# Layer 1's heads: eight state places, early rows, and gated rows and gates on other DMA queues

## The chip, the core and the metric

The kernel runs on one core of one Trainium2 chip. The metric is device time in microseconds, the median of several executions of the whole program. Five engines have a queue of instructions each, worked off in order: PE (TensorE), DVE (VectorE), ACT (ScalarE), POOL (GpSimd) and SP (SyncE, which in this kernel only issues DMAs). A DMA is issued by an instruction in one of the queues of SP, ACT or POOL.

## The reference

Two layers over 640 tokens: 512 of a new stream (the prompt) and 8 running streams of 16 (the sample). Layer 0 is stick-breaking attention, layer 1 gated linear attention (GLA) with four heads and, for each sample stream, a state that is read, used and written back. What matters here is layer 1:

```python
def gla_chunk(S, inp):
    q, k, v, g = inp
    b = jnp.cumsum(g, axis=1)
    b_last = b[:, -1]
    q_in = q * jnp.exp(b)
    a = jnp.einsum('bchd,bshd->bhcs', q_in, k * jnp.exp(-b))
    a = jnp.where(jnp.tril(jnp.ones((C, C), dtype=bool)), a, 0.0)
    o = jnp.einsum('bhcs,bshe->bche', a, v) + jnp.einsum('bchd,bhde->bche', q_in, S)
    S = jnp.exp(b_last)[..., None] * S + jnp.einsum('bshd,bshe->bhde', k * jnp.exp(b_last[:, None] - b), v)
    return S, o

def gla_mixer(h, w_in, w_a2, b_a, g_out, w_out, S0=None):
    q, k, v, r, a_lr = jnp.split(h @ w_in, [nk, 2 * nk, 2 * nk + nv, 2 * nk + 2 * nv], axis=-1)
    g = (jax.nn.log_sigmoid((a_lr @ w_a2 + b_a).astype(f32)) / GLA_TAU).reshape(B, T, GLA_HEADS, GLA_DK)
    S, o = lax.scan(gla_chunk, S0, ...)
    o = o * lax.rsqrt(jnp.mean(o * o, axis=-1, keepdims=True) + EPS) * g_out
    y = (o.reshape(B, T, nv) * jax.nn.silu(r.astype(f32))).astype(h.dtype) @ w_out
    return y, S.astype(h.dtype)
```

`w_out` is 2048 x 2048; a head gives 4 x 128 of its 2048 input rows.

## The kernel before, in words

Products are fp32 in three matmuls: both operands are split into a high and a low part (`halves`, L134 and L135: an ACT cast, then a DVE subtraction), and high x high, high x low and low x high are summed in PSUM. Only the stage of layer 1's heads changes, about 1964 to 2412 us of the span.

**What sets the order.** PE's order is written by the program as it is built: a modelled clock `pe["now"]` moves on with each matmul, and class `Side` weaves side lanes (Python generators) into a main stream. A lane yields `step(wait, tp, z, tiled)`: it goes on when the modelled clock has passed `wait` and the PSUM banks that it asks for are free; `side.after(wait, f)` calls `f` later by that clock; `until` advances the clock till a condition holds. So modelled microseconds decide where an instruction stands, and the chip decides how long it waits there. The other engines' queues follow the order of the calls, rearranged by a scheduler.

**Main stream of the stage.** `others` (L653) makes q and k of heads 1 to 3 in 12 pieces of 128 columns; ACT copies them out of PSUM (L1514, tile `pl`) and stores them (L1516). Then `share(g)` (L699) for g = 0 and 1 is the part of the output projection for head g: 4 column blocks x 5 token blocks, each with 4 rows `kt` and three matmuls a row, added up in tiles `y` (ACT copies at L707 for g = 0, DVE additions at L704 for g = 1). Behind the stage come the rest of the projection (L368) and L2004.

**The side lanes.** `decays` makes the decay factors of each head (L1638 on). `prompt_lane` runs 16 units (head, block of 128 tokens). `sample_lane` treats a head's eight states in four groups of four (dt, e): four products with the states (L1864, into `ps_z`), then for each state a product of keys and values (L1870) with which DVE updates the state (L1872); `leaves` stores the updated state (POOL), and 7 modelled us later `ask` loads the next wanted state into a free place (POOL, tile `s0`, printed `s`). There are `S0` = 7 places. A group's products are written 13 modelled us after the load of its last state was issued, or later.

**Gated rows.** At the end of a unit, and of a head's sample part, `leave` turns the normed result (four transposes, L1601), multiplies it with the gate r on DVE (L1602, in place in the gate's tile) and stores it to the DRAM tensor `og_d` (POOL, L78, printed `og<-gate`). Gates come from DRAM into the same tiles (POOL, `gate<-gr`), two places for the prompt, one for the sample. `fetches` reads the stored rows back, 128 x 640 for each `kt` (SP, tile `og_in`), and splits them into `ogh` and `ogl`; `share(g)` starts when the four rows of head g are split (`came["rows"]`). It asks for the first row once head 0 is through and the last q/k product has been copied out (`came["last"]`).

All POOL DMAs go through `move` (L78) and all SP DMAs through `load` (L71).

Of the kernel before, what the change touches and what calls it, by code (L numbers as in the profile page):

```python
# [8 lines left out]
F32 = mybir.dt.float32  # L9
F32R = mybir.dt.float32r  # L10
# [22 lines left out]
WR = 2  # L33
S0 = 7
GP = 2
# [6 lines left out]
def hybrid_step_kernel(ctx: ExitStack, tc: tile.TileContext, A: dict, O: list):  # L42
# [234 lines left out]
    class Side:  # L277
# [10 lines left out]
        def after(self, wait, what):  # L288

            self.due.append((pe["now"] + wait, what))  # L290
            self.due.sort(key=lambda x: x[0])

        def share(self, **bufs):
            self.free = {k: [0.0] * n for k, n in bufs.items()}
# [389 lines left out]

    def share(g, og, w, leave=None, at=None, first=None):

# [27 lines left out]

        w0, w1 = made(), made()
        for c in range(4):
# [786 lines left out]

    with tc.tile_pool(name="gl", bufs=1, reuse_waits="tile") as gl:
        came = {"plain": False, "last": False, "of": 0, "when": 0.0}

        def keep(dst, hh):
            t = []

            def leave(nt, pt):  # L1510
# [4 lines left out]
                if nt:  # L1515
                    nc.scalar.dma_start(out=dst[:, hh, :], in_=t[0])  # L1516
                    for h in range(1, GH):
                        if hh and dst is gk_d[h]:
# [5 lines left out]
                                 for n0, dst in ((256 * h, gq_d[h]), (NK + 256 * h, gk_d[h])) for hh in range(2)],  # L1524
                       lambda: came.update(plain=True))
        for _ in range(2):
# [28 lines left out]

        masked = [gl.tile([P, P], F32, name=f"aT{n}") for n in range(3)]
        for t in masked:
# [28 lines left out]
        def gate(h, t0, tag, bufs):  # L1586
            g = gl.tile([P, 4, P], F32, tag=tag, name="gate", bufs=bufs)
            move(g, gr_d[h][:, :, t0:t0 + P])
            return g
# [6 lines left out]

        def leave(h, t0, on, g):

            tp = bank("tp")
            for s in range(4):  # L1600
                turn_block(tp[:, P * s:P * s + P], block(on[:, P * s:P * s + P]), ident)  # L1601
            dve.tensor_tensor(g, tp.rearrange("p (s t) -> p s t", s=4), g, op=ALU.mult)  # L1602
            move(og_d[h][:, :, t0:t0 + P], g)

# [4 lines left out]
        def decays():  # L1609

            def weights(h):
                wa2 = gl.tile([96, 256], F32R, tag="wa2", name="wa2", bufs=2)
                load(wa2.bitcast(F32), wa2_d[:, 256 * h:256 * h + 256])
                yield step(4.0 if h else 8.0)
                return wa2
# [54 lines left out]
        def prompt_lane():  # L1670
# [25 lines left out]
            def leave_left():  # L1696
                nonlocal left
                u, on = left
                left = None
                h, c = units[u]  # L1700
                leave(h, P * c, on, gs.pop(u))
                side.after(5.0, lambda: fetch_gate(u + GP))
                if c == 3:
                    through["p"] = h + 1

# [93 lines left out]
        def sample_lane():  # L1799
# [12 lines left out]
            for h in range(GH):  # L1812
# [43 lines left out]
                for n in range(4):  # L1856
                    dt, e = n // 2, n % 2
                    group = [(h, e, dt, m) for m in range(4)]
                    while any(x not in states for x in group):
                        yield step(0.3)  # L1860
                    yield step(max(since, max(states[x][1] for x in group) + 13.0) - pe["now"], tiled=True)
                    for m in range(4):
# [17 lines left out]
                yield step(7.0, tp=1)  # L1880
                leave(h, NP, on, g)
                through["s"] = h + 1
                if h + 1 < GH:
                    yield step(4.0)
                    here = fetch(h + 1)

        def fetches():

            def free(kt):
                g, s = kt // 4, kt % 4  # L1890
                return came["plain"] and came["shares"] >= min(2, g if s > 1 else g - 1)

# [5 lines left out]

            for kt in range(10):
                while min(through.values()) <= kt // 4 or not came["last"]:  # L1900
                    yield step(0.5)
                if kt not in rows:
                    yield step(5.0)
                    ask_rows(kt)
                    if kt % 4 < 3 and kt < 9 and came["plain"]:
                        ask_rows(kt + 1)
                    yield step(4.0)
                while not free(kt):
                    yield step(0.3)
                n = 20 + 2 * kt % 12  # L1910
                og1[kt] = slot(n, name="ogh"), slot(n + 1, name="ogl")
                halves(*og1[kt], rows.pop(kt))
                if kt % 4 < 3 and kt < 9 and kt + 1 not in rows:
                    ask_rows(kt + 1)
                came["rows"], came["at"] = kt + 1, pe["now"]
                yield step(0.5)
# [4 lines left out]
        drive(others)  # L1921
        with tc.tile_pool(name="w4", bufs=1, reuse_waits="tile") as w4:
            ring3["pool"] = w4
            first = [wraw(w_of(0, 0, i), 2, 512) for i in range(2)]
            for g in range(2):
                side.until(lambda: came["rows"] >= 4 * g + 4 and pe["now"] > came["at"] + 2.0)
                drive(share(g, og1, w_out1, first=first))
                came["shares"] = g + 1
                first = [wraw(w_of(g + 1, 0, i), 2, 512) for i in range(2)]
            ring3["pool"] = None  # L1930
            parts = [split(r) for r in first]
            first = [wraw(w_of(3, 0, i), 2, 512) for i in range(2)]
            side.finish()

# [98 lines left out]
```

## Time and profile before

| | us |
|---|---|
| median of 3 runs | 2536.63 (2534.4 to 2538.53) |
| the profiled execution's own time | 2535.51 |
| its span | 2533.8 |
| the stage of layer 1's heads | 1964 to 2412 |
| PE matmuls L653, L699, L1864 (busy, in the stage) | 294.5, 191.8, 21.9 |
| DMA issues on POOL in the stage: s, s stored, gate, og | 64, 64, 20, 20 |

A row of waits reads "engine, what it was about to do, what ended the wait: us in total, times, longest". A row of the timeline reads "start, duration, engine, line, operation, out<-in, shapes, count", with the idle time ahead of it in brackets and what ended it. A row of a table by windows gives the window, its length, the busy time of PE, PE's weight loads, DVE, ACT and POOL with the number of instructions, then the granted TensorE clock (1.00 is full), the share of the 16 DMA engines that was busy, and GB/s.

### The profile page before, as it was taken

The numbers are of one execution on the slowest core, as the hardware profiler recorded it, in microseconds if no ns is written. First come the engines' busy times: TensorE is split into PE (matmuls) and PEld (weight loads), VectorE is DVE, ScalarE is ACT, GpSimd is POOL, SyncE is SP. The second block draws the span as 40 slices with busy tenths as digits, with TensorE's granted clock in tenths as the row PEclk, the third lists the DMA queues.
The fourth block names the chain that finished last, engine by engine and source line by source line (L and its number), as shares of the span: only waits on it lengthen the run. The fifth ranks groups of instructions, "written<-read, shape, count | busy, mean of one in ns | idle before, by whom it ended". The sixth has DMA issues, their size and how long they took to land. (4 is left out here: it accounts for less than half of the span.)

```text
span 2533.8 us, 43960 instructions
## 1 busy us (share of the span) xinstructions
PE 2429.8 (96%) x17561; PEld 2150.1 (85%) x17561; DVE 1581.8 (62%) x2565; ACT 995.2 (39%) x1730; POOL 163.6 (6%) x390
## 2 busy tenths in 40 slices
PE   7899999999999989999999989999999999979998
PEld 5589999999999989888887768999999988857776
DVE  5575555555656655766775678666676565555556
ACT  4342222222223334555442345333333554545223
POOL 0010000000000000000000000000000233342100
PEclk8899999999999999999999999999999999989999
DMA  9966666766654357777864655354434778785634
GB/s 346 327 209 212 223 214 198 241 218 205 219 186 123 113 187 233 260 246 243 267 209 124 214 172 169 96 148 123 125 105 119 212 238 255 217 278 184 228 111 147
DMA packets 469439, 503.13 MB, mean 199 GB/s; under 512 B 42730, under 2 KB 366450, under 8 KB 469106
## 3 DMA queue, kind: packets, MB, share of 16 engines
q1 hardware_dynamic: 446274, 436.60, 54.8%
q0 software_dynamic: 16048, 51.92, 6.1%
q10 hardware_dynamic: 6912, 11.80, 1.3%
q8 instruction: 138, 2.26, 0.4%
q14 instruction: 67, 0.55, 0.1%
HBM read 411.10 MB, written 89.13 MB: 197 GB/s over the span
## 5 line engine op out<-in xcount | busy, mean ns | idle before, releaser
L594 PE MATMUL ps_mm<-sums,wh 128*128 128x320 f32 x2752 | 613.7, 311 | 1.5 <-ACT wh L134 1.5
L594 PE MATMUL ps_mm<-h,wh 128*128 128x320 f32 x2064 | 461.8, 312 | 5.7 <-DVE u L600 4.6
L594 PEld LDWEIGHTS ps_mm<-sums,wh 128*128 128x128 f32 x2752 | 458.3, 188 | 10.4 <-issue 7.4
L594 PE MATMUL ps_mm<-sums,wl 128*128 128x320 f32 x1376 | 425.8, 309 | 0.7 <-DVE wl L135 0.7
L135 DVE TENSOR_TENSOR wl<-wr,wh 128x1024 fp32r<-128x1024 f32 x193 | 236.1, 1224 | 244.0 <-ACT wh L134 243.2
L594 PEld LDWEIGHTS ps_mm<-h,wh 128*128 128x128 f32 x2064 | 343.2, 188 | 21.8 <-issue 13.0
L134 ACT CAST wh<-wb 128x1024 fp32r<-128x1024 f32 x170 | 178.4, 1049 | 426.1 <-PE ps_mm L594 352.8
L134 ACT CAST wh<-wr 128x1024 fp32r<-128x1024 f32 x193 | 202.6, 1050 | 346.6 <-PE ps_mm L594 184.6
L594 PE MATMUL ps_mm<-h,wl 128*128 128x320 f32 x1032 | 319.2, 309 | 0.0
L653 PE MATMUL ps_mm<-h,wh 128*128 128x320 f32 x1152 | 265.2, 318 | 5.3 <-ACT pl L1514 3.1
L594 PEld LDWEIGHTS ps_mm<-sums,wl 128*128 128x128 f32 x1376 | 258.4, 188 | 1.0 <-DVE wl L135 1.0
L135 DVE TENSOR_TENSOR wl<-wb,wh 128x1024 fp32r<-128x1024 f32 x170 | 207.9, 1223 | 60.5 <-ACT wh L134 60.1
L653 PEld LDWEIGHTS ps_mm<-h,wh 128*128 128x128 f32 x1152 | 193.0, 189 | 21.7 <-issue 11.4
L699 PE MATMUL ps_mm<-wh,ogh 128*128 128x512 f32 x450 | 197.4, 439 | 4.2 <-DVE y L704 2.7
L594 PEld LDWEIGHTS ps_mm<-h,wl 128*128 128x128 f32 x1032 | 193.8, 188 | 0.0
L653 PE MATMUL ps_mm<-h,wl 128*128 128x320 f32 x576 | 178.5, 310 | 0.0
L699 PE MATMUL ps_mm<-wh,ogl 128*128 128x512 f32 x450 | 177.9, 395 | 0.3 <-DVE ogl L135 0.3
L699 PE MATMUL ps_mm<-wl,ogh 128*128 128x512 f32 x450 | 177.7, 395 | 0.0
L699 PEld LDWEIGHTS ps_mm<-wh,ogh 128*128 128x128 f32 x450 | 85.6, 190 | 29.6 <-issue 14.4
L653 PEld LDWEIGHTS ps_mm<-h,wl 128*128 128x128 f32 x576 | 108.8, 189 | 0.0
L699 PEld LDWEIGHTS ps_mm<-wh,ogl 128*128 128x128 f32 x450 | 85.0, 189 | 20.3 <-DVE ogl L135 0.7
L518 PE MATMUL ps_mm<-wh,h 128*128 128x512 f32 x252 | 93.4, 432 | 5.9 <-ACT h L134 2.8
(355 smaller groups left out, 3747.0 us busy)
## 6 DMA issues: line engine op xcount, KB each, us to landing
ar<-in_w_ada_dram SPq DMA_DIRECT2D x160, 512.0 KB
wb<-in_sb_w_in_dram SPq DMA_DIRECT2D x82, 512.0 KB
kc<-in_cache_sb_k_dram SPq DMA_DIRECT2D x64, 512.0 KB
vc<-in_cache_sb_v_dram SPq DMA_DIRECT2D x64, 512.0 KB
wr<-in_gla_w_in_dram SPq DMA_DIRECT2D x51, 512.0 KB
wb<-in_gla_w_in_dram SPq DMA_DIRECT2D x45, 512.0 KB
wr<-in_sb_w_in_dram SPq DMA_DIRECT2D x44, 512.0 KB
ar<-in_w_ada_dram SPq DMA_DIRECT2D x64, 256.0 KB
```

The costliest lines, as they stand in the source:

```text
L134: nc.scalar.copy(hi, x)
L135: (e or dve).tensor_tensor(lo, x, hi.bitcast(F32), op=ALU.subtract)
L518: mm(acc[a], l, by(l, r[:, e, :]), start=j == 0 and e == 0 and begun, stop=j == 7 and e == 1 and last)
L594: mm(acc, l[:, k, :], by(l[:, k, :], r), start=start and k == 0 and first, stop=k == 7 and last, skip_group_check=True)
L653: mm(acc[nt], l[:, k, :], by(l[:, k, :], r), start=k0 == 8 and k == 0 and first, stop=k0 == 0 and k == 7 and last)
L699: mm(acc, l, by(l, r[:, e, :]), start=i == 0 and e == 0 and first, stop=i == 1 and e == 1 and last)
```

## The change

1. `S0` is 8. The wait for a group is 9 modelled us after the load for 13, and its `tiled` step (which keeps a distance to other such steps) comes after the wait, in a step of its own.
2. `leave` stores the gated rows from ACT's queue, 2 modelled us after the multiply; what followed the store (the next gate, `through`) follows it still. Gates are loaded from SP's queue. POOL keeps the states, `vst` and `S`.
3. Rows 0 to 2 of head 0 are loaded 8 modelled us after head 0 is through, into the tiles of pool `w4` (row 2 in two parts), and split once all but the last piece of `others` is written. Row 3 and on are read as before, with slightly other waits.
4. `share(0)` is begun at that same point: its weights are loaded and the first half split there (`apart`), the second half when the share goes on.
5. To make room, two of the three tiles `aT` lie in buffers that have served, and `wa2` has one buffer for two.

```diff
@@ -31,7 +31,7 @@
 ZSCALE = 128 ** -0.5
 TOK = T // P
 WR = 2
-S0 = 7
+S0 = 8
 GP = 2
 NPAIR = HEADS // 2
 PLAIN = 2
@@ -682,7 +683,7 @@
 
     y_t = {}
 
-    def share(g, og, w, leave=None, at=None, first=None):
+    def share(g, og, w, leave=None, at=None, first=None, apart=False):
 
 
         src = w.rearrange("(kt p) n -> p kt n", p=P)
@@ -712,7 +713,10 @@
         def made():
             return [t.rearrange("p (a n) -> p a n", a=2) for t in split(raws.pop(0))]
 
-        w0, w1 = made(), made()
+        w0 = made()
+        if apart:
+            yield
+        w1 = made()
         for c in range(4):
             ws = [w0, w1]
             if c < 3:
@@ -1501,7 +1505,8 @@
         k0 = 4 * g + 2 * i
         return w_out1.rearrange("(kt p) n -> p kt n", p=P)[:, k0:k0 + 2, 512 * c:512 * c + 512]
 
-    with tc.tile_pool(name="gl", bufs=1, reuse_waits="tile") as gl:
+    with tc.tile_pool(name="gl", bufs=1, reuse_waits="tile") as gl, \
+            tc.tile_pool(name="w4", bufs=1, reuse_waits="tile") as w4:
         came = {"plain": False, "last": False, "of": 0, "when": 0.0}
 
@@ -1522,7 +1527,7 @@
 
         others = plain(h2, src, [(n0 + P * hh, keep(dst, hh)) for h in range(1, GH)
                                  for n0, dst in ((256 * h, gq_d[h]), (NK + 256 * h, gk_d[h])) for hh in range(2)],
-                       lambda: came.update(plain=True))
+                       lambda: upper())
@@ -1553,7 +1558,7 @@
             for n, (a, b) in enumerate(((0, 0), (0, 1), (1, 0))):
                 mm(out, l[a], by(l[a], r[b]), start=start and n == 0, stop=stop and n == 2, skip_group_check=True)
 
-        masked = [gl.tile([P, P], F32, name=f"aT{n}") for n in range(3)]
+        masked = [t[1].rearrange("p k r -> p (k r)")[:, :P] for t in (sh_t, sc_t)] + [gl.tile([P, P], F32, name="aT2")]
@@ -1585,7 +1590,7 @@
 
         def gate(h, t0, tag, bufs):
             g = gl.tile([P, 4, P], F32, tag=tag, name="gate", bufs=bufs)
-            move(g, gr_d[h][:, :, t0:t0 + P])
+            load(g, gr_d[h][:, :, t0:t0 + P])
             return g
 
         def values(h, a, tag, bufs):
@@ -1594,13 +1599,17 @@
                 load(v[e].bitcast(F32), gv_d[h][e][P * a:P * a + P, :])
             return v
 
-        def leave(h, t0, on, g):
+        def leave(h, t0, on, g, then):
 
             tp = bank("tp")
             for s in range(4):
                 turn_block(tp[:, P * s:P * s + P], block(on[:, P * s:P * s + P]), ident)
             dve.tensor_tensor(g, tp.rearrange("p (s t) -> p s t", s=4), g, op=ALU.mult)
-            move(og_d[h][:, :, t0:t0 + P], g)
+
+            def out():
+                nc.scalar.dma_start(out=og_d[h][:, :, t0:t0 + P], in_=g)
+                then()
+            side.after(2.0, out)
 
 
         ready, through = {}, {"p": 0, "s": 0}
@@ -1698,10 +1707,12 @@
                 u, on = left
                 left = None
                 h, c = units[u]
-                leave(h, P * c, on, gs.pop(u))
-                side.after(5.0, lambda: fetch_gate(u + GP))
-                if c == 3:
-                    through["p"] = h + 1
+
+                def then():
+                    side.after(7.0, lambda: fetch_gate(u + GP))
+                    if c == 3:
+                        through["p"] = h + 1
+                leave(h, P * c, on, gs.pop(u), then)
 
             def scores(u):
 
@@ -1858,7 +1869,8 @@
                     group = [(h, e, dt, m) for m in range(4)]
                     while any(x not in states for x in group):
                         yield step(0.3)
-                    yield step(max(since, max(states[x][1] for x in group) + 13.0) - pe["now"], tiled=True)
+                    yield step(max(since, max(states[x][1] for x in group) + 9.0) - pe["now"])
+                    yield step(0.0, tiled=True)
                     for m in range(4):
                         l = qz[e][:, dt, 32 * m:32 * m + 32]
                         mm(o[32 * m:32 * m + 32, :], l, by(l, states[group[m]][0]), start=False, stop=n == 3,
@@ -1878,17 +1890,46 @@
                 on = normed(o)
                 on = scaled_by(*on)
                 yield step(7.0, tp=1)
-                leave(h, NP, on, g)
-                through["s"] = h + 1
+                leave(h, NP, on, g, lambda: through.update(s=h + 1))
                 if h + 1 < GH:
-                    yield step(4.0)
+                    yield step(9.0)
                     here = fetch(h + 1)
+
+        begun = []
+
+        def upper():
+            came.update(plain=True)
+            begun.append(share(0, og1, w_out1, first=[wraw(w_of(0, 0, i), 2, 512) for i in range(2)], apart=True))
+            next(begun[0])
+
+        def row(kt):
+            n = 20 + 2 * kt % 12
+            og1[kt] = slot(n, name="ogh"), slot(n + 1, name="ogl")
+            return og1[kt]
 
         def fetches():
 
             def free(kt):
                 g, s = kt // 4, kt % 4
-                return came["plain"] and came["shares"] >= min(2, g if s > 1 else g - 1)
+                return came["shares"] >= min(2, g if s > 1 else g - 1)
+
+            while min(through.values()) < 1:
+                yield step(0.5)
+            yield step(8.0)
+            x = [w4.tile([P, 1024], F32, tag=t, name="og_in") for t in ("wh", "wl")]
+            for n in range(2):
+                load(x[n][:, :T], og_d[0][:, n, :])
+            load(x[0][:, T:], og_d[0][:, 2, :1024 - T])
+            load(x[1][:, T:2 * T - 384], og_d[0][:, 2, 1024 - T:])
+            while not came["plain"]:
+                yield step(0.3)
+            for kt in range(2):
+                halves(*row(kt), x[kt][:, :T])
+                yield step(0.8)
+            to = row(2)
+            halves(*[t[:, :1024 - T] for t in to], x[0][:, T:])
+            halves(*[t[:, 1024 - T:] for t in to], x[1][:, T:2 * T - 384])
+            came["rows"], came["at"] = 3, pe["now"]
 
             rows = {}
 
@@ -1896,20 +1937,19 @@
                 rows[kt] = gl.tile([P, T], F32, tag="pl", name="og_in", bufs=2)
                 load(rows[kt], og_d[kt // 4][:, kt % 4, :])
 
-            for kt in range(10):
+            for kt in range(3, 10):
                 while min(through.values()) <= kt // 4 or not came["last"]:
-                    yield step(0.5)
+                    yield step(0.3)
                 if kt not in rows:
-                    yield step(5.0)
+                    if kt > 3:
+                        yield step(5.0)
                     ask_rows(kt)
-                    if kt % 4 < 3 and kt < 9 and came["plain"]:
+                    if 3 < kt < 9 and kt % 4 < 3:
                         ask_rows(kt + 1)
                     yield step(4.0)
                 while not free(kt):
                     yield step(0.3)
-                n = 20 + 2 * kt % 12
-                og1[kt] = slot(n, name="ogh"), slot(n + 1, name="ogl")
-                halves(*og1[kt], rows.pop(kt))
+                halves(*row(kt), rows.pop(kt))
                 if kt % 4 < 3 and kt < 9 and kt + 1 not in rows:
                     ask_rows(kt + 1)
                 came["rows"], came["at"] = kt + 1, pe["now"]
@@ -1919,18 +1959,16 @@
         for x in (decays(), prompt_lane(), sample_lane(), fetches()):
             side.add(x)
         drive(others)
-        with tc.tile_pool(name="w4", bufs=1, reuse_waits="tile") as w4:
+        for g in range(2):
+            side.until(lambda: came["rows"] >= 4 * g + 4 and pe["now"] > came["at"] + 2.0)
             ring3["pool"] = w4
-            first = [wraw(w_of(0, 0, i), 2, 512) for i in range(2)]
-            for g in range(2):
-                side.until(lambda: came["rows"] >= 4 * g + 4 and pe["now"] > came["at"] + 2.0)
-                drive(share(g, og1, w_out1, first=first))
-                came["shares"] = g + 1
-                first = [wraw(w_of(g + 1, 0, i), 2, 512) for i in range(2)]
-            ring3["pool"] = None
-            parts = [split(r) for r in first]
-            first = [wraw(w_of(3, 0, i), 2, 512) for i in range(2)]
-            side.finish()
+            drive(share(g, og1, w_out1, first=first) if g else begun[0])
+            came["shares"] = g + 1
+            first = [wraw(w_of(g + 1, 0, i), 2, 512) for i in range(2)]
+        ring3["pool"] = None
+        parts = [split(r) for r in first]
+        first = [wraw(w_of(3, 0, i), 2, 512) for i in range(2)]
+        side.finish()
 
 
     share_banks(mm=8)
```

Left out: the one buffer of `wa2`, and a second sort in `Side.after` that changes nothing.

Three places where the order of the instructions moves. **PE, at the end of `others`** (`s_...` are states, `qz` queries, `vst` and `kst` values and keys of the sample, `on` a normed result, `wh`/`ogh` the high parts of weights and rows). Before:

```order
L653 MATMUL ps_mm<-h,wl 128x320
L1870 MATMUL ps_tp<-vst,kst_20578 128x512 x3
L1601 MATMUL ps_tp<-ident,on 128x128 x4
L1638 MATMUL ps_tp<-alr_in,wa_22802 128x320 x2
L1864 MATMUL ps_z<-s_23356,qz_20577 32x512
L1864 MATMUL ps_z<-s_23378,qz_20577 32x512
L1864 MATMUL ps_z<-s_23402,qz_20577 32x512
L1864 MATMUL ps_z<-s_23486,qz_20577 32x512
L1870 MATMUL ps_tp<-vst,kst_20579 128x512
L699 MATMUL ps_mm<-wh,ogh 128x512
L699 MATMUL ps_mm<-wl,ogh 128x512
```

With the change:

```order
L700 MATMUL ps_mm<-wh,ogh 128x512
L700 MATMUL ps_mm<-wl,ogh 128x512
L700 MATMUL ps_mm<-wh,ogl 128x512
L700 MATMUL ps_mm<-wh,ogh 128x512
L700 MATMUL ps_mm<-wl,ogh 128x512
L700 MATMUL ps_mm<-wh,ogl 128x512
L1876 MATMUL ps_z<-s_23266,qz_20579 32x512
L1876 MATMUL ps_z<-s_23329,qz_20579 32x512
L1876 MATMUL ps_z<-s_23347,qz_20579 32x512
L1876 MATMUL ps_z<-s_23370,qz_20579 32x512
L700 MATMUL ps_mm<-wh,ogh 128x512
L700 MATMUL ps_mm<-wl,ogh 128x512
```

Before, the group of states stood between the transposes of a prompt unit and the share's first products; now 15 share products stand ahead of it.

**POOL, around the states of head 2's last group** (`out_dram<-s` stores an updated state, `s_...<-in_state_gla_dram` loads one). Before:

```order
L78 DMA out_dram<-s_23227 128x512
L78 DMA gate<-gr_106 128x4x128
L78 DMA out_dram<-s_23339 128x512
L78 DMA og_93<-gate 512x1x128
L78 DMA s_23486<-in_state_gla_dram 128x512
L78 DMA s_23492<-in_state_gla_dram 128x512
```

With the change:

```order
L78 DMA out_dram<-s_22768 128x512
L78 DMA out_dram<-s_22783 128x512
L78 DMA s_23396<-in_state_gla_dram 128x512
L78 DMA out_dram<-s_22793 128x512
L78 DMA s_23411<-in_state_gla_dram 128x512
L78 DMA s_23440<-in_state_gla_dram 128x512
L234 TENSOR_TENSOR on_r<-on_ms,mhalf 128x1
```

The gates and the stores of gated rows are gone from between the states' stores and loads.

**ACT, at the last copies of q and k** (`pl<-ps_mm` is such a copy, `gk_102<-pl` its store). Before:

```order
L1514 COPY pl<-ps_mm 128x320
L1639 ACTIVATE b<-ps_tp,cols 128x320
L1516 DMA gk_102<-pl 128x640
L1639 ACTIVATE b<-ps_tp,cols 128x320
L1642 ACTIVATE b<-b 128x640
L134 CAST ogh<-og_in 128x640
```

With the change:

```order
L1519 COPY pl<-ps_mm 128x320
L1584 ACTIVATE on,oss<-ps_tp 128x512
L1857 CAST kst_20581<-ps_tp 48x512
L1521 DMA gk_102<-pl 128x640
L1766 ACTIVATE ps_tp<-ps_tp,ed 128x512
L1610 DMA og_93<-gate 512x1x128
L1588 ACTIVATE on<-ps_tp,on_r 128x512
L708 COPY y<-ps_mm 128x512
L134 CAST ogh<-og_in 128x640
L1648 ACTIVATE b<-ps_tp,cols 128x320
L1610 DMA og_93<-gate 512x1x128
```

Two stores of gated rows (L1610) now stand in this stretch, and copies of the share's first results (`y`, L708) stand ahead of and between the parts of the decays (`b`).

More of the change, by code (lines that the diff above doesn't have):

```diff
@@ L290, in after @@
             self.due.append((pe["now"] + wait, what))
+            self.due.sort(key=lambda x: x[0])
             self.due.sort(key=lambda x: x[0])
@@ L1611, in weights @@
             def weights(h):
-                wa2 = gl.tile([96, 256], F32R, tag="wa2", name="wa2", bufs=2)
+                wa2 = gl.tile([96, 256], F32R, tag="wa2", name="wa2")
                 load(wa2.bitcast(F32), wa2_d[:, 256 * h:256 * h + 256])
```

## The prediction

> **What bounds the kernel now.** I read the page first, then PE's waits in the changed stage, PE's timeline at the two long ones, the clock there, and last the queue that was late. The page:
>
> ```profile
> span 2533.8 us, 43960 instructions
> ...
> PE 2429.8 (96%) x17561; PEld 2150.1 (85%) x17561; DVE 1581.8 (62%) x2565; ACT 995.2 (39%) x1730; POOL 163.6 (6%) x390
> ```
>
> PE sets the time: 96% busy, 104 us idle. The change issues the same 15303 matmuls, so it can win idle time and time at a lowered clock, no more. What PE waited for from the heads of layer 1 to the end:
>
> ```profile
> PE ps_z L1864 <- DMA s<-in_state_gla_dram: 23.4, 3, 17.4
> PE ps_mm L653 <- ACT pl L1514: 3.1, 2, 1.6
> PE ps_tp L1566 <- DVE k L1664: 1.6, 1, 1.6
> PE ps_mm L368 <- DVE y L704: 1.5, 1, 1.5
> ```
>
> One wait stands out, that of the state products (L1864) for a sample state: 23.4 us in three pieces. The two that matter, in PE's timeline:
>
> ```profile
> 2170.20 1.92 PE L1864 MATMUL ps_z<-s,qz 128*32 128x512 f32 x2 [5.69 <-DMA s<-in_state_gla_dram]
> ...
> 2245.82 1.06 PE L1864 MATMUL ps_z<-s,qz 128*32 128x512 f32 x6
> 2264.32 1.92 PE L1864 MATMUL ps_z<-s,qz 128*32 128x512 f32 x2 [17.44 <-DMA s<-in_state_gla_dram]
> ```
>
> At 2245.82 three products of head 2's last group run and the fourth stands 17.44 us. Idle has a second price, the clock (column PEclk, ahead of the DMA share):
>
> ```profile
> 2168.00:2172.00 4.00, 1.80 (x2) 0.18 (x2) 0.82 (x1) 0.15 (x1) 1.07 (x2) 0.50 0.87 291
> 2172.00:2176.00 4.00, 4.00 (x19) 3.81 (x19) 1.64 (x5) 2.30 (x5) 1.03 (x2) 0.67 0.05 19
> 2248.00:2252.00 4.00, 0.00 (x0) 0.00 (x0) 2.92 (x5) 3.56 (x4) 1.48 (x3) 0.72 1.00 362
> ...
> 2264.00:2268.00 4.00, 3.68 (x6) 1.68 (x7) 0.81 (x2) 0.69 (x2) 0.75 (x1) 0.50 0.75 261
> 2268.00:2272.00 4.00, 4.00 (x14) 3.19 (x13) 2.34 (x4) 1.93 (x3) 2.12 (x4) 0.72 0.35 133
> ```
>
> Work done at a lowered clock costs its busy time times what is missing: 1.80 x 0.50 + 4 x 0.33 = 2.2 us behind the first wait, 3.68 x 0.50 + 4 x 0.28 = 3.0 behind the second. The waits and their shadows hold 23.4 + 5.2 = 28.6 us.
>
> Why the state was late stands in POOL's timeline:
>
> ```profile
> 2161.30 0.72 POOL L78 DMA_DIRECT2D og<-gate  x1 [6.08 <-DVE y L1640]
> ...
> 2251.60 0.76 POOL L78 DMA_DIRECT2D gate<-gr  x1 [1.57 <-issue]
> ...
> 2258.89 0.72 POOL L78 DMA_DIRECT2D og<-gate  x1 [5.99 <-DVE ogl L135]
> 2259.53 1.68 POOL L78 DMA_DIRECT2D s<-in_state_gla_dram  x3
> 2262.42 0.54 POOL L78 DMA_DIRECT2D s<-in_state_gla_dram  x1 [1.21 <-issue]
> ```
>
> The missing state is the first of the three loads at 2259.53. Ahead of it POOL held the store of gated rows 5.99 us; the earlier wait has the same picture (6.08). And it could not be asked sooner: with seven places and groups of four, a group's fourth state needs the place that the first state of the group before gives up.
>
> **The change, part by part.** Transfers of this stage (size, median us to landing):
>
> ```profile
> s<-in_state_gla_dram POOLq DMA_DIRECT2D x64, 256.0 KB, 4.8
> out_dram<-s POOLq DMA_DIRECT2D x64, 256.0 KB, 3.8
> ...
> gate<-gr POOLq DMA_DIRECT2D x20, 256.0 KB, 5.2
> og<-gate POOLq DMA_DIRECT2D x20, 256.0 KB, 3.8
> ```
>
> *Eight places.* The path from a freed place to its next state: update 0.75 (DVE, the row at 2267.00 below), issue 0.55 (POOL, 0.54 at 2262.42), store 3.8, issue 0.55, load 4.8: 10.4 us. With seven places, one of four states of a group has only the time from the previous group's updates to the next products, about 3.8 us on PE at head 2. With eight, a whole group is loaded while the other is used, and the distance is the time between groups. PE's new order puts 17 to 19 us of its own work (an estimate: its rows counted, at the durations of before) between the last update that frees a place of head 2's or 3's last group and that group's products: 7 to 9 us in hand. I take both big waits as gone, and what is left of the third kind (a few tenths to 5 us) as **1**, bounds 0 to 5. The shorter modelled wait (9 for 13) moves products forward and spends part of this margin; it is in that bound. What is late next is the work that stood behind the product:
>
> ```profile
> 2247.79 0.69 DVE L1602 TENSOR_TENSOR gate<-ps_tp,gate 128x512 f32<-128x512 f32 x1
> ...
> 2249.30 0.82 DVE L135 TENSOR_TENSOR ogl<-og_in,ogh 128x640 fp32r<-128x640 f32 x1
> ...
> 2261.14 0.83 DVE L135 TENSOR_TENSOR ogl<-og_in,ogh 128x640 fp32r<-128x640 f32 x1 [0.70 <-ACT ogh L134]
> ...
> 2267.00 0.75 DVE L1872 SCALAR_TENSOR_TENSOR s<-s,es,ps_tp 128x512 f32<-128x512 f32 x1 [4.83 <-PE ps_tp L1870]
> ```
>
> The fourth row of head 0, which the first out-projection products need, was split only at 2261.14 + 0.83 = 2261.97. Without the next part the big wait would shrink by 2264.32 - 2261.97 = 2.3 us and turn into a wait for rows.
>
> *Early rows and the early first weights.* The way of before's first row begins in SP's timeline:
>
> ```profile
> 2243.47 0.32 SPq L71 DMA_DIRECT2D og_in<-og  x1
> ```
>
> Three of the four rows are loaded and split before the last plain product; only row 3 comes on the old path. Between the last q/k product, which lets row 3 be asked, and its first use the new order has about 8.5 us of PE work (counted the same way), and the first row of before took from 2243.47 (issue) to 2249.30 + 0.82 = 2250.12 (split), 6.65 us: 1.9 us in hand.
>
> ```profile
> L135 DVE TENSOR_TENSOR wl<-wr,wh 128x1024 fp32r<-128x1024 f32 x193 | 236.1, 1224 | 244.0 <-ACT wh L134 243.2
> ...
> L134 ACT CAST wh<-wr 128x1024 fp32r<-128x1024 f32 x193 | 202.6, 1050 | 346.6 <-PE ps_mm L594 184.6
> ```
>
> The first weights' conversion lies under others, the second is made once the share resumes, for 1.05 on ACT and 1.22 on DVE; with the copies of y that ACT now makes beside the decays of head 3 I take **2** for the start of the share, bounds 0 (ACT and DVE are 39% and 62% busy) to 6.65 (row 3 late by its whole path).
>
> *Stores of gated rows on ACT, gates on SP.* POOL loses 20 + 20 issues of about 0.73 and 0.76, some 30 us, and what it stood before them:
>
> ```profile
> POOL gate L78 <- DMA og<-gate: 18.5, 6, 5.0
> ...
> POOL og L78 <- DVE gate L1602: 9.8, 7, 4.1
> POOL og L78 <- issue: 6.7, 4, 4.4
> POOL og L78 <- DVE y L1640: 6.1, 1, 6.1
> POOL og L78 <- DVE ogl L135: 6.0, 1, 6.0
> POOL og L78 <- DVE s L1872: 2.2, 1, 2.2
> ```
>
> 30.8 us before the stores and 18.5 before gates, 49.3 in all. Of the stores, ACT now issues each and stands until the multiply has ended. Queued behind it on ACT: copies of q and k and of y out of PSUM (PE needs the bank), conversions of weights, scales of states. The store is written 2.0 modelled us after the multiply, so that ACT mostly finds it done; at the big wait the multiply ended at 2247.79 + 0.69 = 2248.48, 10.4 us before POOL's store. I take **1** for ACT, bounds 0 (never in PE's way) to 30.8 (every hold passed on). For a gate SP stands until the old rows have landed; behind it are rows of v, weights and og rows, asked several us before use. I take **1**, bounds 0 to 18.5. No gain below nothing: PE waited for no gate and no og store elsewhere than counted.
>
> The Trainium skill ("Trainium Kernel Development and Optimization", section "Key Constraints") speaks against this part: DMAs of the SP, ACT and POOL queues run on the same 16 DMA engines, and issuing from several saves only the sequencer's issue time. The DMA share of 1.00 in the row at 2248 agrees that the engines were full there; by this rule the third part is worth its issues alone. Another page, "DMA: Bandwidth & Descriptors", section "SWDGE vs HWDGE vs iDMA", says that GpSimd's descriptor rings are SBUF state that VectorE can lock it out of; POOL's 5.99 us with the multiply long done would fit, and then the move frees POOL of more than its issues; no run here separates the two.
>
> *The tail.* Of the share's products 195 lie behind the last gated row, 213 before.
>
> ```profile
> 2397.42 13.23 PE ps_mm L699 x56
> ```
>
> At 13.23 / 56 = 0.236 us each that is 18 x 0.236 = 4.2 us less cover; PE starts the next section on weights and y, not on that row, with 1.5 us of waiting. I take 0, bounds 0 to 4.
>
> **Sum.** 28.6 - (1 + 2 + 1 + 1) = 23.6 us. Against the profiled run's 2535.5 (span 2533.8; the median is 1.1 higher): **2512**. About 0.2%, 5 us, is what a measurement here can tell from no change.
>
> **Rivals.**
>
> *A transfer limit.* At the big wait the engines were full (share 1.00), and the change takes no byte away; it starts 8 instead of 7 loads at once and adds early rows. If the transfers themselves are the limit there, the big wait stays in another form (a state, a row or weights that land late), and only the first wait goes, where the share was 0.87: 5.7 + 2.2 of clock = 7.9, so 2535.5 - 7.9 = **2528**. For it: the share. Against it: the missing state was asked late, not brought slowly (2259.53 to 2264.32 is 4.8, the median of all 64).
>
> *It does not do what it says.* The wait 13 to 9 moves the products forward by 4 modelled us, as much as a group's distance; if they then meet the same late loads, the eighth place is spent and the waits stay: 2535.5 - 0 = **2535**. Against it: PE's order shows the 17 to 19 us.
>
> *Slower.* The store on ACT is one instruction in a strict queue: it holds copies out of PSUM, and PE stands without a bank. The price is POOL's holds, handed to ACT and SP: 49.3 us. At full price 2535.5 - 28.6 + 49.3 = **2556**. It decides (slower than before by 0.2%) once more than 28.6 + 5 = 33.6 of the 49.3 reaches PE. For it: PE did wait for ACT's copies (L653, 3.1). Against it: most of POOL's holds stood for work that was late for POOL's place in the program only.
>
> **How the numbers follow.** Forecast 0.64, transfer limit 0.20, no effect 0.06, slower 0.10. The range: below, all four new costs at nothing, 2535.5 - 28.6 = 2506.9, and 2 for the runs' spread: 2505. Above, 2528 of the transfer limit and 2 for the runs' spread: 2530, which also holds the forecast with half of SP's bound or half of ACT's passed on (2512 + 9, 2512 + 15); beyond lie 0.16 of the other cases and a little of these two. Faster: 0.64 and 0.19 of the transfer limit, 0.83; same 0.07; slower 0.10.
>
> **What would show it.** Right: the row PE L1864 (now L1876) <- DMA s falls from 23.4 to under 5; no stretch near 2250 at clock 0.50; POOL's issue gaps of 6 us gone; 8 loads land before their group. Wrong: a new row PE <- ACT pl or y of more than 5 us (the slower rival), PE <- DVE ogl near the share's start (row 3 late), the state wait again with a landing above 10 us (the transfer limit), or the time at the median before.

## The result, and the profile after

The changed kernel takes **2514.0 us** (median of 4 runs, 2510.3 to 2514.8) against 2535.9 for the kernel before (median of 4): 0.9909 of it, 95% interval 0.9894 to 0.9924. That is 0.9% faster, 2 us beside the 2512 forecast and inside its range. The profiled execution took 2514.76.

The page of the changed kernel, span and busy time:

```profile
span 2513.0 us, 43986 instructions
...
PE 2427.7 (97%) x17561; PEld 2150.1 (86%) x17561; DVE 1580.6 (63%) x2566; ACT 994.1 (40%) x1731; POOL 135.2 (5%) x350
```

PE's waits from the heads of layer 1 to the end:

```profile
PE ps_mm L654 <- ACT pl L1519: 6.3, 1, 6.3
PE ps_mm L700 <- ACT y L708: 3.8, 2, 1.9
PE ps_mm L369 <- DVE y L705: 1.5, 1, 1.5
```

The row of the state products, 23.4 us before, is gone altogether. In PE's timeline, the group that had stood 17.44 us, and the stretches of the clock there:

```profile
2249.31 2.03 PE L1876 MATMUL ps_z<-s,qz 128*32 128x512 f32 x8
```

```profile
2248.00:2252.00 4.00, 4.00 (x18) 1.72 (x17) 2.53 (x4) 3.20 (x6) 1.09 (x2) 1.00 1.03 408
2252.00:2256.00 4.00, 4.00 (x20) 3.25 (x19) 3.10 (x8) 2.97 (x8) 1.08 (x2) 1.00 1.04 406
```

All eight products run in one go, PE is busy for the whole 4 us at full clock, and the 16 DMA engines are as full (1.03, 1.04) as when PE stood still.

To set the stage apart from the rest I take the time from its first q/k product that waited (1975.36 before, 1979.79 after) to the first product of L368/L369 (2413.01, 2392.24): **437.65 us before, 412.45 after**, 25.2 less. That the profiled executions differ by 20.75 comes of the part ahead of it, which the change does not touch: in the 14 profiled executions of this study that point lies anywhere from 1970.9 to 1979.8. In what follows this stage time stands beside the medians. PE in the stage, before and after:

```profile
1975.36:2413.01 437.65, 404.97 (x2292) 344.54 (x2293) 247.54 (x421) 213.82 (x390) 126.78 (x218) 0.97 0.73 230
1979.79:2392.24 412.45, 399.36 (x2292) 342.73 (x2293) 245.89 (x422) 212.34 (x391) 98.67 (x178) 0.99 0.76 244
```

For the same 2292 matmuls PE is idle 13.1 us where it was idle 32.7, 19.6 less, and busy 5.6 us less, at a mean clock of 0.99 for 0.97.

### The profile page after: what moved, and what is told of

Read it like the earlier page. It is cut to its first block, busy times and chain, and to the rows that moved or that the text cites. A ratio compares the mean times of both kernels' runs of the same rounds, so it can differ in the third digit from the quotient of the medians.

```text
span 2513.0 us, 43986 instructions
## 1 busy us (share of the span) xinstructions
PE 2427.7 (97%) x17561; PEld 2150.1 (86%) x17561; DVE 1580.6 (63%) x2566; ACT 994.1 (40%) x1731; POOL 135.2 (5%) x350
## 4 chain that ended last, share of the span: by engine, by line
PE 78%; DMA 6%; DVE 4%; ACT 3%; issue 1%; SPq 0%; POOL 0%; ACTq 0%; POOLq 0%; DVEq 0%
PE ps_mm L595 40%; PE ps_mm L700 9%; PE ps_mm L654 9%; PE ps_mm L369 3%; PE ps_tp L1086 2%; DMA gv<-kr 2%; PE ps_tp L1559 2%; PE ps_mm L519 1%; PE ps_tp L1046 1%; PE ps_tp L1138 1%; PE ps_z L1022 1%; PE ps_z L180 1%; PE ps_mm L2042 1%; PE ps_z L1100 1%; PE ps_z L222 1%
## 5 line engine op out<-in xcount | busy, mean ns | idle before, releaser
L595 PEld LDWEIGHTS ps_mm<-sums,wh 128*128 128x128 f32 x2752 | 457.9, 188 | 10.4 <-issue 7.4
```

The lines of the kernel that those rows point to most:

```text
L595: mm(acc, l[:, k, :], by(l[:, k, :], r), start=start and k == 0 and first, stop=k == 7 and last, skip_group_check=True)
```

## The experiments

All twelve in one table, with the two kernels. "Gates, og" is the queue of the gate loads and of the stores of gated rows; "wait" the modelled time from load to state products; "rows" whether rows 0 to 2 of head 0 are read early. Each ratio is to runs of the kernel before taken beside it, whose medians went from 2535.9 to 2539.2; so rows are better compared by their ratios than by their medians.

| kernel | places | gates, og | wait | rows | median us | ratio, 95% interval | stage us |
|---|---|---|---|---|---|---|---|
| before | 7 | POOL, POOL | 13 | late | 2535.9 | | 437.65 |
| changed | 8 | SP, ACT | 9 | early | 2514.0 | 0.9909 [0.9894, 0.9924] | 412.45 |
| e1 | **7** | SP, ACT | 9 | early | 2540.5 | 1.0000 [0.9991, 1.0009] | 440.27 |
| e2 | 8 | **POOL, POOL** | 9 | early | 2511.7 | 0.9893 [0.9876, 0.9909] | 414.46 |
| e3 | 8 | SP, ACT | 9 | **late** | 2525.1 | 0.9945 [0.9932, 0.9957] | 425.80 |
| e4 | 8 | POOL, POOL | 13 | late | 2543.4 | 1.0016 [1.0005, 1.0027] | 450.11 |
| e5 | 7 | SP, ACT | 13 | late | 2538.5 | 1.0001 [0.9991, 1.0012] | 441.80 |
| e6 | 8 | SP, ACT | 13 | late | 2539.9 | 1.0007 [0.9998, 1.0016] | 442.84 |
| e7 | 8 | POOL, POOL, later | 13 | late | 2534.6 | 0.9990 [0.9980, 0.9999] | 435.24 |
| e8 | 8 | **first 3 POOL, then SP**; ACT | 9 | early | **2505.3** | 0.9870 [0.9854, 0.9886] | 404.30 |
| e9 | 8 | POOL, ACT | 9 | early | 2515.1 | 0.9912 [0.9899, 0.9926] | 415.62 |
| e10 | e8 again | | | | 2505.2 (1 run) | | 408.52 |
| e11 | e8's | e8's | **13** | early | 2515.2 | 0.9916 [0.9900, 0.9932] | 417.34 |
| e12 | e8's | e8's, og 2 later | 9 | early | 2507.6 | 0.9888 [0.9873, 0.9903] | 413.20 |

My theory was the prediction's: the places end the state waits, the rows keep the hole from filling with the next wait, the queues matter little. Rivals: the queue move alone does it; the transfers are the limit.

**e1, seven places.**

```diff
-S0 = 8
+S0 = 7
```

> The changed kernel with seven state places for eight. If the eighth place is what took the state waits away (the forecast's reason), PE waits for DMA s at the state products again, 5 us or more in all, and the time rises from 2514 to 2519 or more. If the freed POOL queue alone did it (rival), the state waits stay under 1 us and the time within 3 us of 2514.

The whole gain is gone, more than expected, and not at the old place. PE's waits, and its timeline at the end of the stage:

```profile
PE ps_z L1876 <- DMA s<-in_state_gla_dram: 10.8, 4, 4.2
```

```profile
2382.75 1.06 PE L1876 MATMUL ps_z<-s,qz 128*32 128x512 f32 x6
2387.05 1.92 PE L1876 MATMUL ps_z<-s,qz 128*32 128x512 f32 x2 [3.24 <-DMA s<-in_state_gla_dram]
...
2408.53 1.91 PE L1876 MATMUL ps_z<-s,qz 128*32 128x512 f32 x2 [4.24 <-DMA s<-in_state_gla_dram]
...
2416.15 0.79 PE L369 MATMUL ps_mm<-wh,ogh 128*128 128x512 f32 x1 [0.78 <-DVE gate L1607]
```

The share's products are used up at 2382.75; the last three groups of states come behind them, each at the pace of its loads, for 33 us with hardly a product between. With seven places the chain of 64 states is the longest thing in the stage once the share starts sooner.

**e2, both transfers back in POOL's queue.**

```diff
-                nc.scalar.dma_start(out=og_d[h][:, :, t0:t0 + P], in_=g)
+                move(og_d[h][:, :, t0:t0 + P], g)
-            load(g, gr_d[h][:, :, t0:t0 + P])
+            move(g, gr_d[h][:, :, t0:t0 + P])
```

> The changed kernel with the stores of gated rows and the loads of gates back in POOL's queue. If eight places hide POOL's holds (7 to 9 us in hand against holds of up to 6), the state waits stay under 3 us, and the new wait for the copy of q (6.3 us at 2015, ACT's store behind an older DMA) goes with its 1.6 us of clock: 2508 to 2514. If POOL's holds were the cause of the late states whatever the places (rival), 10 us or more of state waits return: 2522 to 2535.

As expected under the theory: no state wait, 2511.7, not to be told from the changed kernel. The three longest rows of PE's waits:

```profile
PE ps_tp L1571 <- DVE k L1673: 4.2, 2, 3.8
PE ps_tp L1606 <- ACT on L1588: 3.1, 1, 3.1
PE ps_mm L654 <- ACT pl L1519: 2.8, 1, 2.8
```

The 6.3 for a copy of q is 2.8 again, and 7.3 us of waits for the heads' work have come in its place. So the queue move as made gains something and gives it back elsewhere; e8 and e9 take that apart.

**e3, late rows.** The early loads are taken out of `fetches` and its loop runs over all ten rows again:

```diff
-            for kt in range(3, 10):
+            for kt in range(10):
```

> The changed kernel with rows 0 to 2 of head 0 read on the old path, after the last plain product; the share is still begun early. If the rows are what stands next behind the states (forecast: split only 16 us after the last plain product), PE waits 10 to 17 us for ogl or the share's start and loses some 3 us to the clock: 2525 to 2534. If the rows were hidden anyway (rival), 2511 to 2517.

PE's waits:

```profile
PE ps_mm L700 <- ACT ogh L134: 15.0, 3, 10.4
```

The rows' own wait came, 15.0 us, and the stage is 13.4 us longer than the changed kernel's: the theory, not the rival.

**e4, the eighth place alone.** The kernel before, with

```diff
-S0 = 7
+S0 = 8
-                wa2 = gl.tile([96, 256], F32R, tag="wa2", name="wa2", bufs=2)
+                wa2 = gl.tile([96, 256], F32R, tag="wa2", name="wa2")
-        masked = [gl.tile([P, P], F32, name=f"aT{n}") for n in range(3)]
+        masked = [t[1].rearrange("p k r -> p (k r)")[:, :P] for t in (sh_t, sc_t)] + [gl.tile([P, P], F32, name="aT2")]
```

> The kernel before with the eighth place alone (and the buffers that make room for it); POOL's queue, rows and waits as before. Forecast's reason: the 5.7 us wait and its 2.2 of clock go, the 17.4 shrinks by 2.3 and becomes a wait for rows: 2535.5 - 10 = about 2525. If the places alone do nothing because POOL's holds set when a state lands (rival): 2533 to 2538, with 15 us or more of waits for DMA s.

Neither: the state waits fell to 0.7 us, and the time did not fall. PE's waits, and POOL's timeline at the longest:

```profile
PE ps_tp L1601 <- ACT on L1583: 26.9, 4, 13.8
```

```profile
2257.64 0.72 POOL L78 DMA_DIRECT2D og<-gate  x1 [2.45 <-issue]
...
2265.36 0.56 POOL L78 DMA_DIRECT2D s<-in_state_gla_dram  x1 [2.17 <-DMA og<-gate]
2265.91 0.56 POOL L78 DMA_DIRECT2D out_dram<-s  x1
2266.49 0.57 POOL L234 TENSOR_TENSOR on_r<-on_ms,mhalf 128x1 f32<-128x1 f32 x1
```

PE now waits for a normed result, whose factor `on_r` POOL makes 0.57 us long behind a line of DMAs that each stood; ACT came to the result at 2268.32, 1.3 us after `on_r` was done. That looked like POOL's queue being the next bound; e6 and e7 were to test it.

**e5, the queue move alone, and e6, eight places and the queue move.** The kernel before with `leave` and `gate` as changed (e5), and with e4's edit as well (e6).

> The kernel before with the queue move alone (gated rows stored from ACT, 2 later, gates loaded from SP; seven places, rows as before). If POOL's hold of 6 us ahead of the late state was its cause (as the prediction read POOL's timeline), the 17.4 shrinks by some 6 us and the 5.7 goes: 2522 to 2530. If the seventh place is the bound (e1 lost the whole gain with the queues moved), the state waits stay above 15 us in all or return elsewhere: 2531 to 2545.

> The kernel before with the eighth place and the queue move, without early rows, early weights and the shorter wait. e4 stood 26.9 us for the normed result, whose factor on_r is made on POOL behind held DMAs. If POOL's queue is the cause, that wait falls under 5 us and what stays is the wait for rows: 2522 to 2532. If eight places cost PE something else (rival), 2538 or more.

Nothing gained in either. PE's waits, of e5:

```profile
PE ps_mm L699 <- ACT ogh L134: 11.0, 2, 7.3
PE ps_mm L653 <- ACT pl L1514: 6.5, 1, 6.5
PE ps_z L1870 <- DMA s<-in_state_gla_dram: 5.0, 4, 2.3
```

and of e6:

```profile
PE ps_tp L1601 <- ACT on L1583: 20.1, 3, 12.8
PE ps_mm L653 <- ACT pl L1514: 4.3, 1, 4.3
```

In e5 the state waits did fall, from 23.4 to 5.0, with seven places. That fits POOL's holds as a cause of the late state, but does not show it alone: the order moved too, and head 2's last group now stands at 2268.36, behind the share's first products. Rows (11.0) and the copy of q took the place of the state waits. In e6 the wait for the normed result stayed with POOL's queue relieved, so **my reading of e4 fell**, as far as POOL was to be the only cause: in e6 `on_r` ended at 2261.3 and ACT came to the result only at 2264.92, behind a row's cast and the decays of head 3.

**e7, as e6 with both transfers in POOL's queue, written later.**

> As e6, but the stores of gated rows and the loads of gates stay in POOL's queue, only written later (2, 7 and 9 modelled us). If the place in POOL's order was what held on_r in e4, this is within 4 us of e6 and the wait for the normed result is under 8 us. If the queue itself is what matters (its gaps put to issue, 100 us in e4 and 5.8 with the change), it is like e4: 2538 to 2546, with 15 us or more of that wait.

Not as either had it: 19.6 us of that wait, as in e6, at 2534.6. Against e4 (26.9, 1.0016) writing the transfers later in the same queue is worth some 7 us by the ratios. In this hole ACT does stand 2.31 us for `on_r`, which ended at 2261.6: here POOL's queue is the last of the chains, in e6 ACT's, and the waits are of one size (12.7 and 12.8).

What e4 to e7 have in common is the place. The long wait behind the last plain product ends at 2264.3 before (a state), 2269.1 in e4 (normed result), 2262.5 in e5 (rows), 2265.7 in e6 and 2262.4 in e7 (normed result); counted from the start of the stage that is 289, 293, 291, 291 and 285 us. It is one hole in PE's program: when q and k are done, PE has no product left that does not hang on head 0's rows, on head 3's decays or on the last unit's result, and whichever of these chains or the state is taken away, the next one ends within some 4 us of it. One thing the four traces share: in the hole ACT stands at the cast of a row of head 0 until the row has landed, 4.11 us in e4 (to 2261.38), 4.73 in e5 (to 2256.36), 2.82 in e6 (to 2261.93) and 3.65 in e7 (to 2250.13), and the decays or the normed result come behind that cast in its queue. So a part of what PE's waits call the normed result is the wait for rows under another name.

The first wait of the kernel before (5.69 at 2170) is gone in e4, e6 and e7 too, but in its place PE stands 6.39, 4.98 and 6.39 us near 2091 for another normed result. Its `on_r` was done 3 to 4 us before ACT came to it, behind the decays of the next head.

**e8, the first three gates from POOL; e10, the same again** (its label names another edit, the kernel is e8's).

```diff
-            load(g, gr_d[h][:, :, t0:t0 + P])
+            (move if h == 0 and t0 in (0, P, NP) else load)(g, gr_d[h][:, :, t0:t0 + P])
```

> The changed kernel with the first three gates of head 0 loaded from POOL as before; all later gates from SP. The changed kernel stood 6.3 us at 2015 for a copy of q: ACT was held 6.7 us at its store of q until an earlier DMA of SP's had landed, behind three more DMAs of SP's. If those three gates are the cause, that wait is about 3 us as before the change, its 1.6 us of clock go, and the time is 2507 to 2512. If it only comes of where the eight state loads fall (rival), the wait stays at 5 to 7 us and the time at 2514.

> A second look at e8, for the trace alone: if its gain over the changed kernel is the start of the stage, the wait for a copy of q near 2007 is 1 to 3 us again and the stage from its first q/k product to the rest of the projection takes 402 to 407 us, where the changed kernel took 412.

The start of the stage in ACT's timeline, first the changed kernel, then e8:

```profile
1995.10 0.42 ACT L1519 COPY pl<-ps_mm 128x320 f32<-128x320 f32 x1
...
2002.59 0.33 ACTq L1521 DMA_DIRECT2D gq<-pl  x1
2002.95 1.28 ACT L1651 ACT_TABLE_LOAD   x1 [7.00 <-DMA v<-gv]
```

```profile
1988.14 0.42 ACT L1519 COPY pl<-ps_mm 128x320 f32<-128x320 f32 x1
...
1988.59 0.33 ACTq L1521 DMA_DIRECT2D gq<-pl  x1
1989.01 1.28 ACT L1651 ACT_TABLE_LOAD   x1
```

ACT's store of q stood until 2002.59 for an older load of v from SP's queue; in e8 it goes at once. The wait for a copy of q is 1.5 us in e8 and 3.8 in e10 (2.3 and 1.5), without a lowered clock behind it. Both came out a little beside what was expected: e8 is under its 2507 to 2512, and e10's stage, 408.52, is over its 402 to 407. The median is 2505.3, and the intervals of e8 and the changed kernel do not meet: **the best version of the study**, 1.3% under the kernel before. Its stage is 4 to 8 us shorter than the changed kernel's (408.52, 404.30 against 412.45), of which the start accounts for 4 to 6.

**e9, all gates from POOL, gated rows still from ACT.**

> The changed kernel with all loads of gates in POOL's queue, the stores of gated rows still on ACT. e2 (both in POOL's queue) gave 2512, e8 (only the first three gates there) 2505. If the gates are what makes POOL's gaps (20 loads in rows of 512 bytes that wait for older DMAs), it stands near e2: 2509 to 2514, with 20 us or more of POOL's idle put to issue. If the stores are, near e8: 2503 to 2508.

POOL's waits, of its loads of gates:

```profile
POOL gate L78 <- DMA og<-gate: 26.3, 6, 6.9
POOL gate L78 <- issue: 22.6, 7, 4.9
```

2515, 1 us above the range for gates as the cause of the gaps, and far from the other: POOL stands 40.4 us "for issue" in all its rows (22.6 of it before gates), against 13 in e8, and the stage is 7 to 11 us longer than e8's. Not all of it is POOL's: the waits for a copy of q are 4.5 us there.

**e11, e8 with the wait of 13 again; e12, e8 with the stores 2 later and the next gate 2 sooner after them.**

```diff
-                    yield step(max(since, max(states[x][1] for x in group) + 9.0) - pe["now"])
+                    yield step(max(since, max(states[x][1] for x in group) + 13.0) - pe["now"])
```

```diff
-            side.after(2.0, out)
+            side.after(4.0, out)
-                    side.after(7.0, lambda: fetch_gate(u + GP))
+                    side.after(5.0, lambda: fetch_gate(u + GP))
```

> e8 with a group's products written 13 modelled us after its last load again, for 9. If the shorter wait brings what the places allow (groups follow each other sooner, so that the last ones end under the share's cover), the last groups of states meet PE without cover and it loses 3 to 15 us: 2508 to 2520. If the wait is only margin (rival), 2503 to 2508.

> e8 with the stores of gated rows written on ACT 4 modelled us after the multiply, for 2, and the next gate 5 after that, for 7. If ACT's hold at the store (2.1 us before a copy of y, PE 1.9 behind it) is what is left of the queue move's price, the waits for y fall from 3.0 to under 1.5 and the time is 2502 to 2505. If it only moves the hold, 2504 to 2508.

e11 lost 10 us, a size that was expected, but not in the way that was expected: no row of PE's waits names a state. The longest is

```profile
PE ps_tp L1854 <- DVE kc L1849: 5.2, 3, 4.2
```

and 4.2 of it stand at 2238.47, in the hole again. ACT's timeline there shows why `kc` is late:

```profile
2236.63 0.72 ACT L134 CAST ogh<-og_in 128x640 fp32r<-128x640 f32 x1 [3.94 <-DMA og_in<-og]
2237.26 0.29 ACT L1848 CAST kc<-kd 128x128 fp32r<-128x128 f32 x1
```

ACT stands 3.94 us for the load of head 1's first row, and `kc` is cast behind it. Why the longer wait moves the order so that this shows was not looked into. All of PE's waits from 1964 on add up to 16.1 us in e11, 7.8 in e8 and 10.5 in e10. e12 gained nothing; its waits for `y` are 3.9 us, and a new one came:

```profile
PE ps_mm L700 <- ACT y L708: 3.9, 3, 1.9
PE ps_tp L1882 <- DVE s L1884: 2.4, 1, 2.4
```

So moving the store does not shorten those waits; what sets them stays open.

## Why the prediction was right, point by point

**The gain of 28.6 us** (waits 23.4, clock 5.2) was right: the row is gone and the clock in that stretch is 1.00. As to its cause, more than one thing would have ended the state waits: the places alone (e4, 0.7 us left) and the queue move alone, with the order that comes with it (e5, 5.0 left), nearly do. Neither shortened the program.

**What is late next** was the step that decided, and it held. Rows split at 2261.97 were to leave 2.3 of the 17.44 us; e4 to e7 end the same hole at 2262 to 2269 and stand between 0.9990 and 1.0016 of the kernel before. Early rows are worth 13.4 us of the stage (e3) with everything else in place. What the step did not see is that the normed result of the last prompt unit and head 3's decays hang in the same place and end as late as the rows. The margin of 1.9 us for row 3 rests on a misread row: the load at 2243.47 is that of head 0's second row; the first was asked at 2233.18 and split at 2243.44, 10.3 us and not 6.65. In the changed kernel row 3 took 8.9 us (asked 2229.26, split 2238.18), and its first product stands at 2240.15, so it was in time by 2.0.

**Eight places: residual 1** (bounds 0 to 5), measured 0. That they were necessary e1 shows, but by another way than the 10.4 us against 3.8: the written order puts the late groups behind the share, and the price is 27.8 us of the stage, not a remainder of the old wait.

**The shorter wait** I treated as a cost inside that bound. It is a gain: e11 puts it at 9 to 13 us of the stage (417.34 against 408.52 and 404.30). The sum takes for granted that nothing new comes late in the hole, and e11 shows that this holds with the wait of 9 and not with 13. By e11 the changed kernel with 13 would stand near 2524, an estimate; neither that kernel, nor early rows, the shorter wait or the early start of the share alone in the kernel before, was tried. That the time came out 2 us from the forecast is in this part luck.

**Start of the share: 2.** PE waits 3.8 for `y` and 0.3 for `wl`, where before it waited 0.9: 3.2.

**ACT 1 and SP 1** were mis-sized, and at a place not thought of. POOL's holds of 49.3 did go to SP:

```profile
SPq L71 <- DMA og<-gate: 99.2, 17, 13.5
```

99.2 us, where POOL stood 18.5 before gates, yet no row of PE's waits names a gate or a gated row. The cost was at the start of the stage, where three gates in SP's queue put ACT's store of q behind a load of v: 6.3 of wait instead of 3.1, and work at a lowered clock behind it:

```profile
2015.10:2019.00 3.90, 3.90 (x17) 3.90 (x18) 2.51 (x5) 3.87 (x5) 0.00 (x0) 0.59 0.44 122
```

3.90 x 0.41 = 1.6, together 4.8 where 2 stood. The sum of the stage by these terms is 28.6 - 3.2 - 4.8 = 20.6, and 25.2 were measured. Of the 4.6 between, 2.0 are the waits for `k` (1.6) and `on` (0.4) of the kernel before, which the new order has lost. Another 2.0 lie in PE's busy time, 5.6 us less where the clock terms give 5.2 - 1.6 = 3.6, and 0.6 in gaps that no row of waits names. The new costs were set too low (8.0 for 5), and what was not counted made up for it: that is luck too.

**The rivals.** *A transfer limit*: refuted by the two windows of the changed kernel above, where the DMA engines are full and PE is busy all the time. *It does not do what it says*: wrong, the longest state wait is gone. *Slower*: the sign set for it, a row PE <- ACT `pl` of more than 5 us, did come (6.3). Its whole price, 4.8, is far under the 33.6 at which that rival decides, and the other handed-over holds stayed off PE's path. The profile counts 17561 matmuls before and after; the prediction's 15303 stands in no view.

By the Trainium skill's rule ("Trainium Kernel Development and Optimization", section "Key Constraints") that issuing from several queues saves only the issue time, the queue move would be worth nothing to PE here. e2 against the changed kernel agrees (2511.7 and 2514.0). With the start mended, e8 is 6 us under e2, where the intervals overlap, and 10 under e9, where they do not; POOL's idle put to issue falls from 53.5 (e2) and 40.4 (e9) to 13. So against e9 moving the gates is worth something to PE; that it is this idle time is not shown, for e5 and e6 have as little of it and gain nothing.

## What to carry to other kernels

Where PE stands with nothing else to do, look for all the chains that end in that hole before valuing the one that the trace names: here the eighth place alone, the queue move alone and the two together gave nothing, and with early rows, the early start of the share and the shorter wait 0.9%. Give the engine work for the hole (early rows), and a longer ring where the ring sets the pace of what comes after. When DMAs move to another queue, look at whose counters they take: a store on ACT stood behind a load that SP had issued.

## What the runs showed of the hardware that was not expected

An ACT store issued in 0.33 us stood 6.7 us (1995.94 to 2002.59) until a load from SP's queue had landed, although it reads nothing of it. The trace keeps the number of the counter (semaphore) at which each DMA reports its landing: in this program those of SP and ACT take 100 to 105, 108 and 109 in turn. The load of v issued at 1986.01 has counter 100 and had landed whole at 2002.52; behind it came three more loads of v, the three gates and a load of weights, and ACT's store, at 2002.59, is the next to take 100. In e8, without the three gates, the store has counter 105, free since 1981.98, and goes at once.

The counter of a DMA can be read for POOL too, where they go from 111 to 118. POOL's gaps that the profile puts to "issue" are 43.6 us in the stage before the change (rows of 15.6, 13.2, 7.9, 6.7 and 0.2), 100.4 in e4, 53.5 in e2, and 5.8 where gates and gated rows are out of its queue (3.5, 1.5, 0.8). The two longest of e4, 5.38 us before a gate at 2178.68 and 5.10 at 2112.21, ended 4.5 and 14.9 us after the last landing at the counters of these DMAs, so it was no older transfer at their own counter that held them; whether another transfer did stays open. The 5.99 us that POOL stood at 2258.89 before the change, with the multiply long done and 16.4 us after the last landing at its counter, has no cause that these runs settle.
